# A decoder block on one core: conditioning in five steps, and products moved from GpSimd to VectorE

## Chip, cores and metric

The kernel runs on one core of a Trainium2 chip. The metric is the device time of one execution in microseconds; less is better. The kernel before takes 2488.12 us (median of three executions, 2487.45 to 2488.19).

## What is computed

One layer of a decoder block on 256 rows of 2048 channels, in float32. A conditioning vector `ada` with nine parts of 2048 comes from one row `c` and a wide weight, and modulates three sub-layers: a SwiGLU network, a token mixer, and a second SwiGLU network.

```python
cond = jax.nn.silu(c)
ada = (cond @ w_ada[l] + b_ada[l]).reshape(B, N_ADA, 1, D)
sh1, sc1, gt1, sh2, sc2, gt2, sh3, sc3, gt3 = [ada[:, i] for i in range(N_ADA)]
h = modulate(x, g_norm[l, 0], sh1, sc1)
x = x + 0.5 * gt1 * swiglu(h, w_ffn_gate[l, 0], w_ffn_up[l, 0], w_ffn_down[l, 0])
u = modulate(x, g_norm[l, 1], sh2, sc2)
q_nsa, kv_nsa, gl_nsa, q_r, k_r, v_r, g_r, ga, gb = jnp.split(u @ w_in[l], split_at, axis=-1)
o_nsa = nsa_attention(q_nsa, kv_nsa, gl_nsa, g_qk[l], cmp_pos[l], cmp_w1[l], cmp_b1[l], cmp_w2[l])
o_ret = retention(q_r, k_r, v_r, g_r, ret_gn_gain[l])
merged = jax.nn.sigmoid(ga) * (o_nsa @ w_proj_nsa[l]) + jax.nn.sigmoid(gb) * (o_ret @ w_proj_ret[l])
x = x + gt2 * (merged @ w_out[l])
h = modulate(x, g_norm[l, 2], sh3, sc3)
x = x + 0.5 * gt3 * swiglu(h, w_ffn_gate[l, 1], w_ffn_up[l, 1], w_ffn_down[l, 1])
```

`modulate` is a root-mean-square norm of each row, times `1 + scale`, plus `shift`. The attention has four groups of four heads with three branches (compressed, selected, window), each a softmax weighted by a gate.

## The kernel before

**Units.** Every weight matrix is read once, in tiles `raw` of 128x1024 (512 KB). A tile is split into a rounded part `whi` (ScalarE, L134) and a remainder `wlo` (VectorE, L135), and the activations into `ahi` and `alo` likewise. One tile with 12 matmuls of 512 columns (hi x hi, hi x lo, lo x hi; two k-tiles; two halves of 128 rows, called half 0 and half 1) is a unit below. `run` (L137) walks one list of items in which weight tiles ("w") and conditioning rows ("a") stand in the order in which SyncE loads them. Six `raw` buffers are in flight (RAW), and items are prepared at most four ahead (AHEAD, PREP). Small pieces of other work stand in the queue `micro`; one is taken after each weight unit. Each engine runs its instructions in the order in which this walk issues them, so a late one holds up what stands behind it.

**Conditioning.** `ada` (L337) multiplies 16 rows of `w_ada` by the elements of `cond` on VectorE (L347, L349), 1024 columns at a time. `ada_cols` (L367) turns the sum into columns of shift and scale. The first network starts in steps (STEPS, `early` at L602): nine chunks of 512 columns run over k-tiles 0 to 3 (18 units), then over k-tiles 4 to 7, and so on; between steps the sums of each chunk are stored (L634) and put back into PSUM (L640) by ScalarE. `first` (L693) makes the conditioning and the modulated activations of a step (`mk`: L736, L737 on ScalarE, L741 on VectorE). `interleave` (L421) spreads the 16 conditioning rows of the next step over the first 95% of a step's units (SPREAD), and `mk` comes after the last of them.

**The norms between the sub-layers.** The last chunk (`tail` in `chunk`, L228) finishes half 0 two units early, so that the row factors of half 0 (L326, GpSimd) are made beside the matmuls of half 1. `norm` (L475) brings them to all partitions by a matmul (L483), multiplies the transposed x (L496 on VectorE for the first 512 channels, L521 on GpSimd for the rest) and makes `ahi` and `alo` (L499, L502, L525, L526). The first two units of the following chunk (HOLD) run on half 0 alone; `head` then makes half 1 and releases their matmuls for half 1. `x_scaled` (L458) transposes 512 channels of x (L454, 8 transposes) and scales them.

**Attention.** For each group the list `steps` at L1097 stands in `micro`. `scores` makes masked scores, `softmax` (L1041) exponentials on ScalarE and, through `weigh` (L967), the product with gate and reciprocal sum on GpSimd (L971, L1050); `c_softmax` (L992) does so for the compressed branch (L998, L1003); `p_tr` (L1053) transposes and splits (L1063, L1064), `pv` (L1068) multiplies by the values (L1078 to L1080).

Of the kernel before, what the change touches and what calls it, by code (L numbers as in the profile page):

```python
# [32 lines left out]
RAW, PREP, AHEAD, T4, T2, EARLY, SPREAD = (6, 4, 4, 6, 8, 9, 0.95)  # L33
# [14 lines left out]
STEPS = ((0, 4), (4, 4), (8, 4), (12, 4))  # L48
# [23 lines left out]
def block_kernel(ctx: ExitStack, tc: tile.TileContext, I, konst, decay, out):  # L72
# [43 lines left out]
    items, micro, held, first_lo = [], deque(), [], []  # L116
# [20 lines left out]
    def run():  # L137
# [11 lines left out]
        def dma():  # L149
            while st["dma"] < len(stream) and (st["dma"] < RAW or st["dma"] - RAW in freed):  # L150
                i = st["dma"]
                _, src, nk, n, _ = stream[i]
# [11 lines left out]
        def prep():  # L164
            i = st["prep"]
            kind, _, nk, n, fn = stream[i]
            raw = raws.pop(i)
            if kind == "w":
                hi = wp.tile([P, 2 * NCH], F32R, tag="whi", name="whi")
                lo = wp.tile([P, 2 * NCH], F32R, tag="wlo", name="wlo")  # L170
                if st["w"]:
                    split(raw[:, :nk * n], hi[:, :nk * n], lo[:, :nk * n])
                else:
                    nc.scalar.activation(hi[:, :nk * n], raw[:, :nk * n], AF.Copy)
                    first_lo.append(lambda: nc.vector.tensor_tensor(
# [10 lines left out]
        at, nw = 0, 0  # L186
        for it in items:
# [4 lines left out]
            if kind == "bar":  # L192
                bars.pop(0)
                continue
            while st["prep"] < len(stream) and st["prep"] <= at + AHEAD and (not bars or st["prep"] < bars[0]):
# [32 lines left out]
    def chunk(act, src, K, n, done, nk=2, banks=accb, head=None, tail=None):  # L228
# [29 lines left out]
        return its[:h0] + ([("bar", HOLD[2])] if head else []) + its[h0:]  # L258
# [108 lines left out]
    def ada_cols(lay, k0, nk=4, first=False):  # L367
# [12 lines left out]
        def done(acc):  # L380
            if first:
# [3 lines left out]
                finish(ps[:, 0:2 * nk].rearrange("p (i k) -> p i k", i=2))  # L385
                return
# [79 lines left out]
    def rstd_diag(t):  # L466
# [3 lines left out]
        rsqrt_mean(r, r, D)  # L470
        dg = t2([P, P])
# [3 lines left out]
    def norm(xa, his, los, dgs):  # L475

        box = []

        def rows_of(t):
            if not t:  # L480
                box.append(mx([P, 2, S])[:, 0])
            r = box[0][:, t * P:(t + 1) * P]
            nc.tensor.matmul(r, ones, dgs[t], start=True, stop=True)  # L483
            return r

        def half(t):
            r = rows_of(t)
            ts = slice(t * P, (t + 1) * P)
            if not t:
                his.append(act_hi())  # L490
                los.append(act_lo())
            h = xa[0]

            def scaled(b):
                hb = h[:, 2 * b:2 * b + 2, ts]
                nc.vector.tensor_tensor(hb, hb, r[:, None, :].to_broadcast([P, 2, P]), op=ALU.mult)  # L496

            def hi(k):
                nc.scalar.activation(his[0][:, k, ts], h[:, k, ts], AF.Identity, bias=mod[:, 0, k:k + 1])  # L499

            def lo(k):
# [191 lines left out]
    def first(k0, nk):  # L693
# [602 lines left out]
```

## Time and profile before

| | before |
|---|---|
| median of three executions | 2488.12 us |
| the profiled execution, its own time | 2489.26 us |
| its span, first to last instruction | 2487.5 us |
| TensorE matmuls busy | 2432.4 us (98%) |
| VectorE busy | 1724.6 us (69%) |
| ScalarE busy | 1202.7 us (48%) |
| GpSimd busy | 233.0 us (9%) |
| moved by DMA | 616.65 MB, mean 248 GB/s |
| mean granted TensorE clock | 0.998 |

The busy share of an engine is a mean over stages with different limits. TensorE's matmuls overlap: each lasts 380 ns and one starts every 0.216 us, so its idle time is read from gaps between starts. The profile gives, for an instruction that waited, the time that its engine sat idle and what ended it.

### The profile page before, as it was taken

How to read it: one execution, taken by the hardware profiler on the slowest of the kernel's cores; microseconds unless marked ns; L12 is line 12 of the kernel's file. 1: busy time of each engine (PE TensorE's matmuls, PEld its weight loads, DVE VectorE, ACT ScalarE, POOL GpSimd, SP SyncE). 2: the span in 40 equal slices, each digit the busy share in tenths (PEclk: the TensorE clock that was granted, in tenths of full speed). 3: DMA queues.
4: the chain of work that ended last, by engine and by line, in shares of the span. 5: the costliest groups of instructions: out<-in, count | busy, mean ns of one | idle time of the engine just before them, and what ended most of it. 6: DMA issues, size and time to landing. Idle time of an engine off the chain costs nothing. (4 is left out here: it accounts for less than half of the span.)

```text
span 2487.5 us, 31657 instructions
## 1 busy us (share of the span) xinstructions
PE 2432.4 (98%) x11614; PEld 2115.6 (85%) x11614; DVE 1724.6 (69%) x1960; ACT 1202.7 (48%) x1550; POOL 233.0 (9%) x206
## 2 busy tenths in 40 slices
PE   6999999999999999999999999999899999999999
PEld 4888888888887888888888888888788888888887
DVE  7887768998756467876666777776688555555555
ACT  4777444444445455564444444444544444444443
POOL 1000000110002133320001101001200010001001
PEclk9999999999999999999999999999999999999999
DMA  9998888899876555667888787876598666666664
GB/s 349 355 354 294 277 293 299 296 319 339 276 228 185 143 146 153 202 207 264 281 267 254 251 258 250 280 267 233 168 332 326 210 203 201 197 201 202 199 202 153
DMA packets 348264, 616.65 MB, mean 248 GB/s; under 512 B 22096, under 2 KB 79926, under 8 KB 347852
## 3 DMA queue, kind: packets, MB, share of 16 engines
q1 hardware_dynamic: 347852, 614.51, 74.9%
q8 instruction: 91, 1.49, 0.3%
q14 instruction: 65, 0.53, 0.1%
q0 software_dynamic: 256, 0.12, 0.0%
HBM read 612.45 MB, written 2.10 MB: 247 GB/s over the span
## 5 line engine op out<-in xcount | busy, mean ns | idle before, releaser
L135 DVE TENSOR_TENSOR wlo<-raw,whi 128x1024 fp32r<-128x1024 f32 x864 | 1076.6, 1255 | 588.0 <-ACT whi L134 582.6
L134 ACT ACTIVATE whi<-raw 128x1024 fp32r<-128x1024 f32 x864 | 907.1, 1057 | 945.7 <-PE accb L221 722.8
L219 PE MATMUL accb<-whi,ahi 128*128 128x512 f32 x3168 | 1213.8, 383 | 5.9 <-ACT ahi L499 5.5
L220 PE MATMUL accb<-wlo,ahi 128*128 128x512 f32 x3168 | 1202.9, 380 | 3.9 <-DVE wlo L135 3.7
L221 PE MATMUL accb<-whi,alo 128*128 128x512 f32 x3168 | 1202.4, 380 | 2.4 <-DVE alo L546 1.1
L219 PEld LDWEIGHTS accb<-whi,ahi 128*128 128x128 f32 x3168 | 599.7, 189 | 90.1 <-ACT ahi L499 6.3
L220 PEld LDWEIGHTS accb<-wlo,ahi 128*128 128x128 f32 x3168 | 599.9, 189 | 89.3 <-DVE wlo L135 7.2
L221 PEld LDWEIGHTS accb<-whi,alo 128*128 128x128 f32 x3168 | 599.6, 189 | 89.3 <-DVE alo L526 1.6
L349 DVE SCALAR_TENSOR_TENSOR aacc<-raw,cond,aacc 128x1024 f32<-128x1024 f32 x270 | 354.9, 1314 | 2.0 <-DMA raw<-in_w_ada_dram 1.0
L563 POOL TENSOR_TENSOR x<-x,t 128x512 f32<-128x512 f32 x50 | 80.9, 1640 | 1383.8 <-DVE t L561 988.0
L622 PE MATMUL accb<-wlo,ahi 128*128 128x512 f32 x288 | 112.8, 392 | 2.5 <-DVE wlo L135 2.5
L623 PE MATMUL accb<-whi,alo 128*128 128x512 f32 x288 | 110.4, 383 | 2.0 <-DVE alo L741 2.0
L621 PE MATMUL accb<-whi,ahi 128*128 128x512 f32 x288 | 110.7, 384 | 0.3 <-ACT whi L134 0.2
L622 PEld LDWEIGHTS accb<-wlo,ahi 128*128 128x128 f32 x288 | 54.8, 190 | 17.5 <-DVE wlo L135 10.3
L623 PEld LDWEIGHTS accb<-whi,alo 128*128 128x128 f32 x288 | 54.8, 190 | 10.4 <-DVE alo L741 3.5
L621 PEld LDWEIGHTS accb<-whi,ahi 128*128 128x128 f32 x288 | 54.9, 191 | 9.3 <-ACT whi L134 0.9
L546 DVE TENSOR_TENSOR alo<-mx,ahi 128x512 fp32r<-128x512 f32 x52 | 33.5, 686 | 29.8 <-ACT ahi L545 29.8
L545 ACT ACTIVATE ahi<-mx 128x512 fp32r<-128x512 f32 x52 | 28.2, 596 | 49.8 <-PE mx L454 49.8
L561 DVE TENSOR_TENSOR t<-accb,gt 128x512 f32<-128x512 f32 x56 | 36.2, 684 | 7.3 <-PE accb L221 7.3
L580 ACT ACTIVATE t<-accb 128x512 f32<-128x512 f32 x44 | 26.1, 599 | 25.6 <-PE accb L221 21.1
L1160 POOL TENSOR_SCALAR rs<-bmv 128x2 f32<-128x2 f32 x8 | 1.8, 221 | 375.8 <-DVE bmv L1159 375.5
L807 ACT ACTIVATE t<-accb 128x512 f32<-128x512 f32 x44 | 25.9, 597 | 22.7 <-PE accb L221 22.7
(202 smaller groups left out, 1094.5 us busy)
## 6 DMA issues: line engine op xcount, KB each, us to landing
raw<-in_w_ada_dram SPq DMA_DIRECT2D x288, 512.0 KB, 5.5
raw<-in_w_ffn_gate_dram SPq DMA_DIRECT2D x176, 512.0 KB, 5.3
raw<-in_w_ffn_up_dram SPq DMA_DIRECT2D x176, 512.0 KB, 4.6
raw<-in_w_ffn_down_dram SPq DMA_DIRECT2D x176, 512.0 KB, 4.4
raw<-in_w_in_dram SPq DMA_DIRECT2D x176, 512.0 KB, 4.5
raw<-in_w_in_dram SPq DMA_DIRECT2D x128, 256.0 KB, 3.8
raw<-in_w_proj_nsa_dram SPq DMA_DIRECT2D x32, 512.0 KB, 5.6
raw<-in_w_proj_ret_dram SPq DMA_DIRECT2D x32, 512.0 KB, 5.4
```

Source lines behind the costliest of these rows:

```text
L134: nc.scalar.activation(hi_ap, raw_ap, AF.Copy)
L135: nc.vector.tensor_tensor(lo_ap, raw_ap, hi_ap.bitcast(F32), op=ALU.subtract)
L219: nc.tensor.matmul(ps[t], xh, wh, start=kt == 0, stop=False)
L220: nc.tensor.matmul(ps[t], xh, wl, start=False, stop=False)
L221: nc.tensor.matmul(ps[t], xl, wh, start=False, stop=kt == K - 1)
L349: nc.vector.scalar_tensor_tensor(box[0], raw, k, box[0], op0=ALU.mult, op1=ALU.add)
L546: nc.vector.tensor_tensor(lo[:, 2 * b:2 * b + 2], ps, h.bitcast(F32), op=ALU.subtract)
L561: nc.vector.tensor_tensor(in_two(y), halves(ps[t]), in_two(gt[:, n * NCH:(n + 1) * NCH]), op=ALU.mult)
L563: (nc.vector if last and n == 3 else nc.gpsimd).tensor_tensor(xs, xs, y, op=ALU.add)
L621: nc.tensor.matmul(ps[t], xh, wh, start=kt + a == 0, stop=False, **kw)
L622: nc.tensor.matmul(ps[t], xh, wl, start=False, stop=False, **kw)
L623: nc.tensor.matmul(ps[t], xl, wh, start=False, stop=kt + a == k0 + nk - 1, **kw)
```

## The change

Four things change. First, the conditioning of the first network goes in five steps of 2, 2, 4, 4 and 4 k-tiles: the first two steps use rows of 512 columns (256 KB) and have nine units each. The rows of a step all come before the last three units of the preceding step (REST), and its shift, scale and activations (`by_ones`, `whole`, `low`) are queued after those last units and after the first unit of the step. The first step's `xs` is scaled for its own k-tiles alone. Second, in the norms all products go to VectorE, by halves and by pairs of k-tiles (`by_row`); three sets of transposes (`x_scaled(1)`, `x_turned(2)`, `x_turned(3)`) stand beside the norm's matmuls; the remainder of the third unit's weights is made after half 1's activations; and five items after it prepare one weight tile each (SLOW). The product by the gate for half 1 (`by_gate`) and its sum with x (`plus`) are separate pieces. Third, the clearing of two tiles (`clear`) goes 60 items forward. Fourth, the softmax products of attention go to VectorE, one step after the exponentials. The diff, cut to its core:

```diff
-RAW, PREP, AHEAD, T4, T2, EARLY, SPREAD = (6, 4, 4, 6, 8, 9, 0.95)
+RAW, PREP, AHEAD, T4, T2, EARLY, REST = (6, 4, 4, 6, 8, 9, 3)
...
-WARM = (10, 15, 4)
+WARM = (9, 12, 4)
...
-POOLN = 0
-O1 = ((0, 0), (0, 1), (1, 0), (1, 1), (1, 2), (1, 3), (2, 0), (2, 1), (2, 2), (2, 3))
-O0 = ((0, 0), (0, 1), (1, 0), (1, 1), (1, 2), (1, 3), (2, 0), (2, 1), (3, 0), (2, 2), (2, 3), (3, 0))
-ORDER = (O0, O1)
+SLOW = 5
 HOLD = (2,2,1)
 LATE = 4
 GAPS = (2, 4, 3, 2)
-STEPS = ((0, 4), (4, 4), (8, 4), (12, 4))
+STEPS = ((0, 2), (2, 2), (4, 4), (8, 4), (12, 4))
...
-                if st["w"]:
+                if st["w"] and len(stream[i]) == 5:
...
+                few = SLOW if len(it) > 2 else 0
...
+                if few and done:
+                    break
+                done += stream[nxt][0] == "w"
                 prep()
+            few = max(few - 1, 0)
...
-        return its[:h0] + ([("bar", HOLD[2])] if head else []) + its[h0:]
+        if head:
+            its[h0] += ("late",)
+        return its[:h0] + ([("bar", HOLD[2], "slow")] if head else []) + its[h0:]
...
-            if first:
+            def by_ones():
                 ps = mx()
                 for k in range(2 * nk):
                     nc.tensor.matmul(ps[:, k:k + 1], acc[:, k * P:(k + 1) * P], ones[:, 0:1], start=True, stop=True)
                 finish(ps[:, 0:2 * nk].rearrange("p (i k) -> p i k", i=2))
+            if then is not None:
+                if k0 == 0:
+                    by_ones()
+                else:
+                    soon(by_ones, *then)
                 return
...
-                    w = interleave(w, first(*STEPS[i + 1]), int(len(w) * SPREAD), *LEAD)
+                    w = interleave(w, first(*STEPS[i + 1]), len(w) - REST, *LEAD)
...
+        def by_row(n, b, t):
+
+            ts = slice(t * P, (t + 1) * P)
+            hb = xa[n][:, 2 * b:2 * b + 2, ts]
+            nc.vector.tensor_tensor(hb, hb, box[0][:, None, ts].to_broadcast([P, 2, P]), op=ALU.mult)
...
+                pending.pop(0)()
+            nc.tensor.matmul(box[0][:, ts], ones, diag(r2[t]), start=True, stop=True)
+            turned[turn] = x_turned(turn)
+            if t:
+                by_row(2, 0, 0)
...
+            for b in range(2):
+                by_row(0, b, t)
+            for k in range(4):
+                nc.scalar.activation(his[0][:, k, ts], xa[0][:, k, ts], AF.Identity, bias=mod[:, 0, k:k + 1])
+            lo(0)
+            lo(1)
+            if not t:
+                pending.pop(0)()
+            lo(2)
+            lo(3)
+            if not t:
+                pending.pop(0)()
+
...
         def at_once():
-            half(0)
+            xa.append(x_scaled(1))
+            half(0, 2)
+            by_row(1, 0, 0)
+            by_row(1, 1, 0)
+            xa.append(x_scaled(2, turned[2]))
             drain()
 
         def head():
-            half(1)
-            rs.append(t2([P, S]))
-            nc.scalar.activation(rs[0], box[0], AF.Copy)
-            push(part(1), part(2), lambda: xa.append(x_scaled(3)), part(3))
+            half(1, 3)
+            part(1, ((0, 1), (1, 1)))()
+            while late_lo:
+                late_lo.pop()()
+            xa.append(x_scaled(3, turned[3]))
+            push(lambda: lo_of(1), part(2, ((1, 0), (0, 1), (1, 1))), lambda: lo_of(2),
+                 part(3, ((0, 0), (1, 0), (0, 1), (1, 1))), lambda: lo_of(3))
         return at_once, head
...
-            pending.append(lambda: add_x(ps, 3, lambda t, n: None, (1,)))
+            y = []
+            pending.append(lambda: y.append(by_gate(ps, 3, 1)))
+            pending.append(lambda: plus(y[0], 3, 1, nc.vector))
...
+        then = [lambda: whole(0, 2), lambda: (low(), whole(2, 2)), low] if nk == 4 else [lambda: whole(0, 2), low]
+        o = ada_cols(0, k0, nk, then)
+        o.insert(12, ("do", turn))
+        o.insert(8, ("do", scaled))
+        if k0 == STEPS[1][0]:
+            o.insert(5, ("do", load_more))
+        return o
...
-                dgs.append(rstd_diag(t))
-            elif t == 1:
+                rs.append(rstd(t))
+            elif t == 1 and n == 0:
                 push(*[None] * GAPS[2], lambda: xa.append(x_scaled(n)))
...
+            items.insert(len(items) - 60, ("do", lambda: clear()))
...
-            nc.gpsimd.tensor_tensor(sums, sums, gate, op=ALU.mult)
+            nc.vector.tensor_tensor(sums, sums, gate, op=ALU.mult)
...
-                nc.gpsimd.tensor_tensor(pv[:, t], pv[:, t], mask_c[:, t, None, :].to_broadcast([P, 4, NCMP]), op=ALU.mult)
+                nc.vector.tensor_tensor(pv[:, t], pv[:, t], mask_c[:, t, None, :].to_broadcast([P, 4, NCMP]), op=ALU.mult)
...
-            nc.gpsimd.tensor_tensor(p3, p3, s8[:, :, None].to_broadcast([P, 8, NCMP]), op=ALU.mult)
+            weigh(sv, gates[:, :, 4 * g:4 * g + 4])
+            nc.vector.tensor_tensor(p3, p3, s8[:, :, None].to_broadcast([P, 8, NCMP]), op=ALU.mult)
...
-                nc.gpsimd.tensor_tensor(s, s, sums[:, :, None].to_broadcast([P, 4, n]), op=ALU.mult)
+                weigh(sums, gates[:, t, c0:c0 + 4])
+                nc.vector.tensor_tensor(s, s, sums[:, :, None].to_broadcast([P, 4, n]), op=ALU.mult)
...
-        steps = [k_tr, None, None, None, q_tr, c_scores, scores(1, 1), both(softmax(1, 1), scores(0, 1)),
-                 both(softmax(0, 1), c_softmax), both(scores(1, 0), scores(0, 0)),
-                 both(p_tr(1, 1), c_split, softmax(1, 0), softmax(0, 0)), None, both(pv(1, (1,), False), p_tr(0, 1)), c_tr,
-                 both(pv(1, (0,), True), p_tr(1, 0), p_tr(0, 0)), None, pv(0, (1, 0), True)]
+        steps = [k_tr, None, None, None, q_tr, c_scores, both(c_exp, scores(1, 1)), both(exps(1, 1), scores(0, 1)),
+                 both(c_norm, weighed(1, 1), exps(0, 1)), both(weighed(0, 1), c_split, scores(1, 0), scores(0, 0)),
+                 both(p_tr(1, 1), exps(1, 0), exps(0, 0)), both(weighed(1, 0), weighed(0, 0)),
+                 both(pv(1, (1,), False), p_tr(0, 1)), c_tr, both(pv(1, (0,), True), p_tr(1, 0), p_tr(0, 0)), None,
+                 pv(0, (1, 0), True)]
```

**ScalarE, end of the step that precedes k-tiles 4 to 7.** L640/L673 puts a chunk's sums back, L634/L667 stores them, L736/L762 and L737/L763 make activations. Before (the last rows of `mk`):

```order
L737 ACTIVATE t_695<-mx,mod 128x256
L736 ACTIVATE ahi<-mx,mod 128x256
L737 ACTIVATE t_695<-mx,mod 128x256
L634 ACTIVATE t_716<-accb 128x512 x2
L134 ACTIVATE whi<-raw 128x1024
L640 ACTIVATE accb<-alo 128x512 x2
L134 ACTIVATE whi<-raw 128x1024
```

In the change:

```order
L673 ACTIVATE accb<-alo 128x512 x2
L667 ACTIVATE ahi<-accb 128x512 x2
L673 ACTIVATE accb<-t_508 128x512 x2
L667 ACTIVATE alo<-accb 128x512 x2
L762 ACTIVATE ahi<-mx,mod 128x256
L763 ACTIVATE t_763<-mx,mod 128x256
L762 ACTIVATE ahi<-mx,mod 128x256
L763 ACTIVATE t_763<-mx,mod 128x256
L131 ACTIVATE whi<-raw 128x1024
L673 ACTIVATE accb<-ahi 128x512 x2
```

Four of the eight activations now stand between the storing of the last chunk but one and the putting back of the first chunk's sums (the L673 row at the end); the other four come after that.

**VectorE, first norm, from half 1's product on.** L496/L501 is the product by the row factors, L502/L516 and L526/L539 make `alo`, L135/L132 and L172 `wlo`. Before:

```order
L496 TENSOR_TENSOR t_5887<-t_5887,mx 128x2x128 x2
L502 SCALAR_TENSOR_TENSOR alo<-t_5887,mod,ahi 128x128 x4
L526 SCALAR_TENSOR_TENSOR alo<-t_6030,mod,ahi 128x256 x4
L135 TENSOR_TENSOR wlo<-raw,whi 128x1024 x3
L526 SCALAR_TENSOR_TENSOR alo<-t_6165,mod,ahi 128x256 x4
L135 TENSOR_TENSOR wlo<-raw,whi 128x1024 x2
L526 SCALAR_TENSOR_TENSOR alo<-t_6385,mod,ahi 128x256 x4
L135 TENSOR_TENSOR wlo<-raw,whi 128x1024 x3
L830 COPY t_6487<-mx 128x512 x2
L837 TENSOR_TENSOR t_6500<-t_6487,cols 128x960
```

In the change:

```order
L516 SCALAR_TENSOR_TENSOR alo<-t_5983,mod,ahi 128x128 x4
L501 TENSOR_TENSOR t_6303<-t_6303,mx 128x2x128 x2
L172 TENSOR_TENSOR wlo<-raw,whi 128x1024
L539 SCALAR_TENSOR_TENSOR alo<-t_6303,mod,ahi 128x256 x4
L132 TENSOR_TENSOR wlo<-raw,whi 128x1024
L501 TENSOR_TENSOR t_6345<-t_6345,mx 128x2x128 x3
L132 TENSOR_TENSOR wlo<-raw,whi 128x1024
L539 SCALAR_TENSOR_TENSOR alo<-t_6345,mod,ahi 128x256 x4
L132 TENSOR_TENSOR wlo<-raw,whi 128x1024
L501 TENSOR_TENSOR t_6403<-t_6403,mx 128x2x128 x4
L132 TENSOR_TENSOR wlo<-raw,whi 128x1024
L539 SCALAR_TENSOR_TENSOR alo<-t_6403,mod,ahi 128x256 x4
```

The products of L521 on GpSimd have become rows of VectorE between the weights' remainders, which now come one at a time.

**VectorE, first group's softmax.** L1034/L1076 makes scores, L1000/L1042 sums the compressed branch, L970/L1010 takes reciprocals, L1098 is the product by gate and sum. Before:

```order
L969 TENSOR_SCALAR s_7411<-s_7411 128x4
L970 RECIPROCAL s_7411<-s_7411 128x4
L1000 TENSOR_REDUCE s_7423<-pc 128x8
L969 TENSOR_SCALAR s_7423<-s_7423 128x8
L970 RECIPROCAL s_7423<-s_7423 128x8
L135 TENSOR_TENSOR wlo<-raw,whi 128x1024
L1034 SCALAR_TENSOR_TENSOR t_7450<-kc,mx 128x128 x4
L1037 TENSOR_REDUCE m_7460<-t_7450 128x4
L1034 SCALAR_TENSOR_TENSOR t_7462<-kc,mx 128x128 x4
L1037 TENSOR_REDUCE m_7472<-t_7462 128x4
```

In the change:

```order
L1040 TENSOR_TENSOR pc<-pc,kc 128x60 x2
L1042 TENSOR_REDUCE s_7498<-pc 128x8
L1009 TENSOR_SCALAR s_7498<-s_7498 128x8
L1010 RECIPROCAL s_7498<-s_7498 128x8
L1011 TENSOR_TENSOR s_7498<-s_7498,gates 128x8
L1045 TENSOR_TENSOR pc<-pc,s_7498 128x120
L1009 TENSOR_SCALAR s_7435<-s_7435 128x4
L1010 RECIPROCAL s_7435<-s_7435 128x4
L1011 TENSOR_TENSOR s_7435<-s_7435,gates 128x4
L1098 TENSOR_TENSOR t_7404<-t_7404,s_7435 128x1024
L132 TENSOR_TENSOR wlo<-raw,whi 128x1024
L1009 TENSOR_SCALAR s_7508<-s_7508 128x4
```

The sum of the compressed branch stood behind a product on GpSimd; now that product (L1040) and those by the gate (L1011, L1045, L1098) are VectorE's own.

## Rows read from the trace of the kernel before

**Rows 1.** The page, busy time, share of the span and instructions.

```profile
PE 2432.4 (98%) x11614; PEld 2115.6 (85%) x11614; DVE 1724.6 (69%) x1960; ACT 1202.7 (48%) x1550; POOL 233.0 (9%) x206
```

**Rows 2.** Busy time by stretch; after POOL: granted clock, DMA share, GB/s.

```profile
10.00:20.00 10.00, 1.36 (x3) 0.55 (x3) 8.17 (x11) 3.80 (x10) 3.04 (x2) 1.00 1.05 387
...
842.00:864.00 22.00, 22.00 (x129) 19.25 (x128) 9.15 (x18) 10.32 (x14) 3.25 (x5) 1.00 0.43 126
```

**Rows 3.** Timeline of the start: start, duration (us), engine, line, [idle before].

```profile
15.50 17.55 DVE L349 SCALAR_TENSOR_TENSOR aacc<-raw,cond,aacc 128x1024 f32<-128x1024 f32 x13
...
33.05 1.06 ACT L174 ACTIVATE whi<-raw 128x1024 fp32r<-128x1024 f32 x1 [9.28 <-DMA raw<-in_w_ffn_gate_dram]
...
33.11 1.95 PE L384 MATMUL mx<-ones,aacc 128*128 128x1 f32 x16 [1.04 <-DVE aacc L349]
...
36.16 0.48 PE L621 MATMUL accb<-whi,ahi 128*128 128x512 f32 x1
```

**Rows 4.** A group of the page: count, busy us, mean ns, idle before.

```profile
L561 DVE TENSOR_TENSOR t<-accb,gt 128x512 f32<-128x512 f32 x56 | 36.2, 684 | 7.3 <-PE accb L221 7.3
```

**Rows 5.** Timeline of ScalarE within and at the end of the second step.

```profile
111.17 1.06 ACT L134 ACTIVATE whi<-raw 128x1024 fp32r<-128x1024 f32 x1 [0.66 <-DMA raw<-in_w_ffn_gate_dram]
112.14 1.10 ACT L640 ACTIVATE accb<-ahi 128x512 f32<-128x512 f32 x2
...
143.04 0.58 ACT L736 ACTIVATE ahi<-mx,mod 128x256 fp32r<-128x256 f32 x1
143.49 0.58 ACT L737 ACTIVATE t<-mx,mod 128x256 f32<-128x256 f32 x1
```

**Rows 6.** TensorE, timeline at two places, and its waits in total (us, times, longest).

```profile
92.75 0.48 PE L623 MATMUL accb<-whi,alo 128*128 128x512 f32 x1 [0.17 <-DVE alo L741]
...
167.93 0.48 PE L622 MATMUL accb<-wlo,ahi 128*128 128x512 f32 x1 [0.63 <-DVE wlo L135]
...
PE accb L623 <- DVE alo L741: 2.0, 3, 1.4
```

**Rows 7.** Timeline of the two norms.

```profile
753.42 1.04 PE L454 MATMUL mx<-kc,x 128*128 128x128 f32 x8
...
769.72 1.23 DVE L135 TENSOR_TENSOR wlo<-raw,whi 128x1024 fp32r<-128x1024 f32 x1 [0.70 <-ACT whi L134]
...
770.87 0.75 DVE L496 TENSOR_TENSOR t<-t,mx 128x256 f32<-128x256 f32 x2
...
771.77 0.80 PE L219 MATMUL accb<-whi,ahi 128*128 128x512 f32 x1 [2.20 <-ACT ahi L499]
...
793.62 0.38 PE L221 MATMUL accb<-whi,alo 128*128 128x512 f32 x1
...
1785.68 0.48 PE L219 MATMUL accb<-whi,ahi 128*128 128x512 f32 x1 [1.41 <-ACT ahi L499]
...
1793.04 1.69 ACT L525 ACTIVATE ahi<-t,mod 128x256 fp32r<-128x256 f32 x4
...
1796.19 1.66 DVE L526 SCALAR_TENSOR_TENSOR alo<-t,mod,ahi 128x256 fp32r<-128x256 f32 x4
...
1807.55 0.38 PE L221 MATMUL accb<-whi,alo 128*128 128x512 f32 x1
```

**Rows 8.** VectorE's waits in total.

```profile
DVE s L1000 <- POOL pc L998: 16.7, 4, 6.6
```

**Rows 9.** Timeline of the first two groups' softmax.

```profile
918.32 0.28 DVE L1000 TENSOR_REDUCE s<-pc 128x8 f32<-128x120 f32 x1 [6.61 <-POOL pc L998]
...
920.20 0.48 PE L220 MATMUL accb<-wlo,ahi 128*128 128x512 f32 x1 [1.24 <-DVE wlo L135]
...
924.96 0.48 PE L1079 MATMUL mx<-t,t 128*128 128x512 f32 x1 [1.90 <-DVE t L1064]
...
987.07 0.48 PE L1079 MATMUL mx<-t,t 128*128 128x512 f32 x1 [1.64 <-DVE t L1064]
```

**Rows 10.** Busy time in the third group's softmax.

```profile
1040.00:1062.00 22.00, 21.70 (x115) 18.67 (x115) 20.38 (x49) 15.70 (x36) 8.85 (x11) 1.00 0.67 205
```

More of the change, by code (lines that the diff above doesn't have):

```diff
@@ L113, in in_two @@
         return ap.rearrange("p (h j) -> p h j", h=2)
-    items, micro, held, first_lo = [], deque(), [], []
+    items, micro, held, late_lo = [], deque(), [], []
     def weights(src, nk, n, fn):
@@ L185, in run @@
         dma()
[L186 removed]
+        at, nw, few = 0, 0, 0
         for it in items:
@@ L365, in over_partitions, with ada_cols @@
         return halves(ps)
-    def ada_cols(lay, k0, nk=4, first=False):
+    def ada_cols(lay, k0, nk=4, then=None):
         ks = slice(k0, k0 + nk)
@@ L473, in rstd_diag, with norm, half @@
         return dg
-    def norm(xa, his, los, dgs):
-        box = []
-        def rows_of(t):
+    def norm(xa, his, los, r2):
+        box, turned = [], {}
+        def by_row(n, b, t):
+            ts = slice(t * P, (t + 1) * P)
+            hb = xa[n][:, 2 * b:2 * b + 2, ts]
+            nc.vector.tensor_tensor(hb, hb, box[0][:, None, ts].to_broadcast([P, 2, P]), op=ALU.mult)
+        def half(t, turn):
+            ts = slice(t * P, (t + 1) * P)
             if not t:
                 box.append(mx([P, 2, S])[:, 0])
[L482 to L489, printed above, removed]
@@ new lines, in half, with hi_of @@
+            for k in range(4):
[8 more added lines that the diff above has]
+                pending.pop(0)()
+        def hi_of(n):
+            his.append(act_hi())
+            for k in range(4):
+                nc.scalar.activation(his[n][:, k], xa[n][:, k], AF.Identity, bias=mod[:, 0, 4 * n + k:4 * n + k + 1])
@@ L528, in part, with lo_of @@
+        def lo_of(n):
+            los.append(act_lo())
+            for k in range(4):
+                nc.vector.scalar_tensor_tensor(los[n][:, k], xa[n][:, k], mod[:, 0, 4 * n + k:4 * n + k + 1],
+                                               his[n][:, k].bitcast(F32), op0=ALU.add, op1=ALU.subtract)
+        def part(n, whats):
+            def f():
+                for b, t in whats:
+                    by_row(n, b, t)
+                hi_of(n)
             return f
-        rs = []
         def at_once():
-            half(0)
+            xa.append(x_scaled(1))
[3 more added lines that the diff above has]
+            xa.append(x_scaled(2, turned[2]))
@@ L1039, in scores, with exps, f, weighed @@
             return f
-        def softmax(br, t):
+        def exps(br, t):
+            def f():
+                s, m = box["p", br, t], box["m", br, t]
+                sums = sp.tile([P, 4], F32, tag="s4", name="s4", bufs=4)
+                for h in range(4):
+                    nc.scalar.activation(s[:, h], s[:, h], AF.Exp, bias=m[:, h:h + 1], accum_out=sums[:, h:h + 1])
+                box["s", br, t] = sums
+            return f
+        def weighed(br, t):
             def f():
                 n = P * (t + 1)
-                s, m = box["p", br, t], box["m", br, t]
-                sums = small(4, "s4")
-                for h in range(4):
-                    nc.scalar.activation(s[:, h], s[:, h], AF.Exp, bias=m[:, h:h + 1], accum_out=sums[:, h:h + 1])
+                s, sums = box["p", br, t], box["s", br, t]
                 c0 = 16 * (1 + br) + 4 * g
-                weigh(s, sums, gates[:, t, c0:c0 + 4], 4)
-                nc.gpsimd.tensor_tensor(s, s, sums[:, :, None].to_broadcast([P, 4, n]), op=ALU.mult)
+                weigh(sums, gates[:, t, c0:c0 + 4])
+                nc.vector.tensor_tensor(s, s, sums[:, :, None].to_broadcast([P, 4, n]), op=ALU.mult)
             return f
@@ L1258, in block_kernel @@
     h3, l3 = [], []
-    at_once, head = norm(xa3, h3, l3, dg3)
+    at_once, head = norm(xa3, h3, l3, r3_)
     items.append(("do", at_once))
```

155 lines of the change are left out of this document (65 added, 90 removed).

## The prediction

> **What bounds the kernel now.** I read the busy line of the page first [rows 1]: TensorE's matmuls fill 98% of the span, so a microsecond saved on another engine counts only where TensorE waits. Next the timeline of TensorE, for gaps between starts: it stands idle for the main work until 36.16 us [rows 3], and then in stalls at the steps' ends [rows 6], at the two norms [rows 7] and in attention [rows 9]. One unit is 12 matmuls, one each 0.216 us, 2.59 us. The sum is made against the profiled execution (2489.26 us), 1.14 us over the median of three (2488.12). Some 0.2% (5 us) is what a measurement can tell from no change.
>
> **The start.** Before the first main matmul come x (2.1 MB) and 16 rows of 0.524 MB; the DMA engines are full there, at 387 GB/s [rows 2], so a row needs 1.355 us. VectorE's products keep that pace, 17.55/13 = 1.35 us each [rows 3]. The last product ends at 33.05; less itself and 27.1 us of loads, loading begins at 4.6. With half as many bytes in rows (4.2 MB) loads end at 4.6 + 16.3 = 20.9. A product of 512 columns has no row; the nearest operation of that size with two inputs takes 684 ns [rows 4], half of the 1.35, so the last one ends at about 22 to 22.6, and the 16 small matmuls (1.95 us, [rows 3]) halve. The first main matmul moves from 36.16 to about 24.7, 11 us earlier.
>
> **What the second step does with it.** The first unit of k-tiles 4 to 7 (unit 19) still needs all rows of k-tiles 0 to 7. Ahead of the last row stand x, 16.8 MB of rows and 17 weight tiles before, 15 after: 27.8 and 26.7 MB, so at the full rate it lands at 4.6 + 71.8 = 76.4 and now at 73.6. With holes, as six buffers come free only behind their users, I take 76. The second step's rows cannot hide: its first six units have 15.5 us of matmuls, and 16 rows with 6 tiles need 22 x 1.355 = 29.8 us. So TensorE waits for transfers. After the last row come its product (1.4), a first tile's landing, rounding and remainder (about 2.5), three units and the small matmuls (2). Per unit ScalarE rounds (0.97, [rows 5]), puts two sums back and stores two (1.05 each, by the 1.10 row), 3.0 us, over the 2.59. Behind the last stores it does four activations at 0.45 [rows 5], a rounding and a putting back before unit 19 can begin, 3.8 us, as its order shows. That makes 76 + 1.4 + 2.5 + 3 x 3.0 + 3.8 = 92.7, and about 93.2 with the first remainder. Before, the same unit started at about 92.5 [rows 6]: **+0.7**. At the full rate, with three units at 2.59 and nothing of ScalarE's 3.8 in the way, it is 73.6 + 1.4 + 2.5 + 7.8 = 85.3, 7.2 us earlier than before: the bound on the good side. At the three boundaries before, the waits for `alo` add up to 2.0 us, and the wait for the weights' remainder beside one adds 0.63 [rows 6]; with activations made over the three units ahead, I estimate 1.3 less in all. **Early part: -0.6.**
>
> On the other side, 256-KB rows have no row in the trace. The slowest nearby stretch moves 126 GB/s at a busy share of 0.43 [rows 2], 293 at full share; 8.4 MB of rows (both steps) at 293 instead of 387 cost 6.9 us. I take nothing, because with six transfers in flight the 512-KB rows already fill the engines. The Trainium skill (DMA: Bandwidth & Descriptors, Measured (HBM→SBUF, 128 partitions, SWDGE, issued from GpSimd)) wants transfers of 1 MiB or more for three quarters of the peak; read between its sizes, 256 KB would do some 62% where 512 KB do 73%, an estimate that costs 3.8 us; no run here shows 256 KB yet.
>
> **The norms.** Two sets of 8 transposes leave TensorE's busy time for idle gaps, about 0.8 us each (row of 753.42, [rows 7]): -1.6 per norm. The third set lies within the next figure. Release: half 1's held matmuls start at 771.77 and 1785.68 [rows 7]. At the first, a weights' remainder (1.23) stands ahead of half 1's products on VectorE; held back now, and with the gate's product in a piece of its own (0.7 sooner), this gives 2.0; at the second norm, where the chain was shorter, about 1.1. After the release: before, unit 8 ended 21.9 us later both times (793.62, 1807.55). Now what GpSimd did beside joins VectorE and alternates with ScalarE. VectorE from the release: lows 1.3, products (0.375 each by [rows 7]) until 2.0, held remainder 3.2, four lows (1.66) 4.9; unit 4's remainder waits until 5.9 for its rounding, behind eight activations on ScalarE (1.69 per four), and ends at 7.1; products 8.2; ScalarE's four activations and a rounding, 10.6; remainder 11.8; lows 13.4; remainder and four products 16.1; activations and rounding 18.8; remainder and lows 21.6; the last unit ends at 24.5. So +2.6. First norm -1.6 - 2.0 + 2.6 = **-1.0**, second -1.6 - 1.1 + 2.6 = **-0.1**; I allow 3 each way, a chain of this length being worth one remainder and one set of lows either way.
>
> **Attention.** VectorE stands 16.7 us in four waits for GpSimd's product of the compressed branch, the longest 6.6 [rows 8]; in the first group it delays a weights' remainder (TensorE waits 1.24) and the transposed softmax (1.90), in the second 1.64 [rows 9]. These waits go. In their place VectorE does the products: two of 128x1024 ahead of the transposes (1.14 each, as a remainder of that size), small ones 1.1, 3.4 us per group, and 4.9 with the later ones. So VectorE comes to the transposes earlier by 4.2 us with the smaller waits in the first group, and by 1.5, 0.5 and 0.6 in the others. Counted by starts, TensorE's gaps there are 1.39 + 2.06, 1.80, 0.71 and some 0.5; they shrink by 3.45, 1.5, 0.5 and 0.5: **-6.0**, between -7 (all gaps) and the rival below.
>
> **Sum.** -0.6 - 1.0 - 0.1 - 6.0 = -7.7: the profiled execution comes to 2481.6, the median to **2480.4 us**.
>
> **Rivals.**
> *The start's gain is kept.* If transfers stay dense and ScalarE keeps up, unit 19 starts 7.2 us earlier and not 0.7 later: 2480.4 - 7.9 = about 2472. For it: 2.7 us less to load, and only 26.7 MB to move by then. Against it: ScalarE's 3.0 us per unit, and its order at the boundary. Chance 0.18.
> *The early part loses.* Smaller rows or a ScalarE that lags cost up to 6.9 us: 2480.4 + 6.9 = about 2487, no change. Chance 0.18. The rule of the Trainium skill above would be one way to it.
> *VectorE fills up in attention* (the other side). In the third group it is busy for 20.38 of 22 us already [rows 10]. If its 4.9 us more per group find no idle time in groups two to four, weights' remainders come late behind them: 3 x 4.9 - 3.45 = +11.3, in place of -6.0, 2480.4 + 17.3 = 2497.7. It decides once VectorE lags more than the four units prepared ahead (10.4 us); +6.7 in attention is enough for slower by 0.2%. Against it: it had idled 16.7 us there, and 0.3 us more in each group does not make a lag of ten. Chance 0.05.
> *The change does not do what it says*: the order shows 512-column rows, the products on VectorE and the moved activations, so I give it nothing of its own.
>
> **Chances and range.** The forecast itself has 0.59; its own range, 2475 to 2486, is the norms' allowance and the early part's smaller errors. Of it 0.49 lies beyond 0.2% and 0.10 within; the first rival is faster, the second 0.02 faster, 0.14 within and 0.02 slower, the third slower. Faster 0.69, same 0.24, slower 0.07. Range **2468 to 2488**: it reaches to both early rivals and leaves out the third.
>
> **What would show it.** Right: the first main matmul at about 24.7; TensorE and DMA waits between it and unit 19, which starts near 93; ScalarE nearly full before; releases at about 2 and 1 us less, and unit 8 ending 24 to 25 us behind them; L1042 with no wait for GpSimd, and no wait of L1127 for the transposed softmax. Wrong: unit 19 under 89 or over 97; unit 8 within 22 us of the release; waits of TensorE for `wlo` in the second to fourth group's softmax.

## The result and the profile after

The change made the kernel slower: 2502.31 us (median of 6; 2500.21 to 2503.86) against 2488.15 (6 runs of the kernel before), a ratio of 1.0051, interval 1.0041 to 1.0061. The forecast was 2480.4, with 2488 as the upper end. The profiled execution took 2502.37 us with a span of 2500.2, 12.7 more than before.

The same step in both traces shows where. The lag of the change behind the kernel before is -9.4 us at the first main matmul (26.77 for 36.16), +13.0 in unit 19, the first of k-tiles 4 to 7 (its first matmul with `alo`: 105.76 for 92.75), +14.4 when the gates of the first network are made (467 us), +15.4 ahead of the first norm and +16.7 behind it, +12.3 behind attention, and +12.4 behind the second norm and at the end. The reading at 467 us is on the low side. Both traces have 10368 main matmuls (those that write `accb`), so the n-th of one can be set beside the n-th of the other. Counted so, the lag is +16.7 us throughout from 210 to 450 us of the kernel before, for example here, first before and then in the change:

```profile
293.11 0.38 PE L219 MATMUL accb<-whi,ahi 128*128 128x512 f32 x1
```

```profile
309.77 0.38 PE L222 MATMUL accb<-whi,ahi 128*128 128x512 f32 x1
```

It falls to +13.9 at 510 us and is back at +15.4 by 589. All runs below gain 0.8 to 2.8 us from 450 to 510, and attention_alone, whose code up to attention is that of the kernel before, gains 2.8 as well; so the fall comes from the one execution of the kernel before and not from the change. The early part lost 16.7 by this count, the first norm 1.3, attention gave back 4.4, and the second norm changed nothing.

The page's busy line and busy time by stretch, columns as in [rows 1, 2]:

```profile
PE 2440.4 (98%) x11610; PEld 2119.7 (85%) x11610; DVE 1744.3 (70%) x2049; ACT 1220.9 (49%) x1586; POOL 170.0 (7%) x146
```

```profile
10.00:20.00 10.00, 4.56 (x9) 2.18 (x10) 8.63 (x16) 3.38 (x10) 1.91 (x2) 1.00 1.03 322
20.00:25.00 5.00, 4.30 (x13) 1.85 (x12) 3.71 (x6) 0.00 (x0) 0.00 (x0) 1.00 0.78 237
25.00:55.00 30.00, 23.86 (x88) 17.55 (x88) 22.04 (x28) 17.73 (x27) 0.00 (x0) 0.89 0.99 330
65.00:75.00 10.00, 6.96 (x28) 4.64 (x26) 9.81 (x9) 7.31 (x14) 0.00 (x0) 1.00 0.83 266
1052.00:1074.00 22.00, 21.79 (x118) 19.00 (x117) 21.04 (x49) 14.87 (x34) 0.00 (x0) 1.00 0.58 170
```

TensorE is busy for 98% as before, and that says nothing. The last two columns do: loading at the start ran at 387 GB/s [rows 2] and now runs at 237 to 330 in these four stretches, with a DMA share of 0.78 to 1.03. Against 387, they lack 0.65 + 0.75 + 1.71 + 1.21 = 4.3 MB, 11.2 us of loading. The kernel before was not at 387 throughout either (352 from 25 to 55 us). From 10 to 90 us it moved 29.75 MB and the change 26.56, 3.2 MB less, which is 8.2 us at 387; first before, then the change:

```profile
DMA packets 15558, 29.75 MB, mean 372 GB/s; under 512 B 926, under 2 KB 1182, under 8 KB 15553
```

```profile
DMA packets 18064, 26.56 MB, mean 332 GB/s; under 512 B 1070, under 2 KB 9173, under 8 KB 18059
```

The timeline of the start, and of the end of the second step (as [rows 3, 5, 6]):

```profile
13.53 10.24 DVE L354 SCALAR_TENSOR_TENSOR aacc<-raw,cond,aacc 128x512 f32<-128x512 f32 x13
23.82 1.05 PE L389 MATMUL mx<-ones,aacc 128*128 128x1 f32 x8 [0.70 <-DVE aacc L354]
26.77 0.79 PE L654 MATMUL accb<-whi,ahi 128*128 128x512 f32 x1 [0.86 <-ACT ahi L762]
...
87.60 1.28 DVE L354 SCALAR_TENSOR_TENSOR aacc<-raw,cond,aacc 128x1024 f32<-128x1024 f32 x1
88.88 1.06 ACT L131 ACTIVATE whi<-raw 128x1024 fp32r<-128x1024 f32 x1 [1.74 <-DMA raw<-in_w_ffn_gate_dram]
...
100.49 0.60 ACT L667 ACTIVATE alo<-accb 128x512 f32<-128x512 f32 x1 [0.70 <-PE accb L656]
100.98 0.56 ACT L762 ACTIVATE ahi<-mx,mod 128x256 fp32r<-128x256 f32 x1
...
102.78 1.07 ACT L131 ACTIVATE whi<-raw 128x1024 fp32r<-128x1024 f32 x1
103.72 1.14 ACT L673 ACTIVATE accb<-ahi 128x512 f32<-128x512 f32 x2
...
104.39 0.48 PE L654 MATMUL accb<-whi,ahi 128*128 128x512 f32 x1 [1.35 <-ACT accb L673]
105.76 0.48 PE L656 MATMUL accb<-whi,alo 128*128 128x512 f32 x1 [0.67 <-DVE alo L768]
```

The last row of k-tiles 4 to 7 is multiplied by 88.9 us, not by 77.4 as forecast; from there to unit 19 the order on ScalarE is the forecast one.

The slow stretch from 65 to 75 us holds no short rows: every transfer issued in it has 512 KB. It stands behind the boundary that the change adds, between its two short steps (unit 10):

```profile
61.51 0.58 ACT L763 ACTIVATE t<-mx,mod 128x256 f32<-128x256 f32 x1
...
63.95 1.09 ACT L131 ACTIVATE whi<-raw 128x1024 fp32r<-128x1024 f32 x1
...
65.08 1.22 DVE L132 TENSOR_TENSOR wlo<-raw,whi 128x1024 fp32r<-128x1024 f32 x1 [2.27 <-ACT whi L131]
```

ScalarE is busy without a gap from 60 to 70 us, with four activations and the sums of that boundary, so the weights' rounding is late; VectorE waits for it with landed rows in line behind, and is then busy for 9.81 of 10 us. Meanwhile buffers come free late, and the DMA share falls to 0.73 (65 to 70).

At the last boundary something comes that was not forecast:

```profile
209.83 0.58 ACT L763 ACTIVATE t<-mx,mod 128x256 f32<-128x256 f32 x1
210.28 2.02 ACT L131 ACTIVATE whi<-raw 128x1024 fp32r<-128x1024 f32 x2
...
211.39 2.36 DVE L132 TENSOR_TENSOR wlo<-raw,whi 128x1024 fp32r<-128x1024 f32 x2 [3.54 <-ACT whi L131]
213.66 0.68 DVE L768 TENSOR_TENSOR alo<-t,ahi 128x512 fp32r<-128x512 f32 x1
214.40 0.79 PE L656 MATMUL accb<-whi,alo 128*128 128x512 f32 x1 [3.43 <-DVE alo L768]
214.99 0.63 PE L654 MATMUL accb<-whi,ahi 128*128 128x512 f32 x1
```

The second pair's activations are done at about 210.3, but their remainder (L768) stands on VectorE behind two weights' remainders, which wait for two roundings behind those activations. TensorE idles 3.43 us, and afterwards a matmul lasts 0.63 us in place of 0.38: the granted clock is 0.83 over 210 to 220, so some 3.4 us at 1.2 GHz.

The norms (TensorE; release and end of unit 8, as [rows 7]) and attention (VectorE, then TensorE, as [rows 8, 9]):

```profile
783.80 0.48 PE L222 MATMUL accb<-whi,ahi 128*128 128x512 f32 x1 [0.47 <-ACT ahi L521]
...
802.24 0.48 PE L222 MATMUL accb<-whi,ahi 128*128 128x512 f32 x1 [1.04 <-ACT whi L131]
...
810.22 0.38 PE L224 MATMUL accb<-whi,alo 128*128 128x512 f32 x1
...
1795.46 0.48 PE L222 MATMUL accb<-whi,ahi 128*128 128x512 f32 x1 [0.47 <-ACT ahi L521]
...
1819.92 0.38 PE L224 MATMUL accb<-whi,alo 128*128 128x512 f32 x1
...
927.70 0.28 DVE L1042 TENSOR_REDUCE s<-pc 128x8 f32<-128x120 f32 x1
...
938.83 0.48 PE L1127 MATMUL mx<-t,t 128*128 128x512 f32 x1 [0.54 <-DVE t L1112]
```

TensorE's wait there in total (us, times, longest):

```profile
PE mx L1127 <- DVE t L1112: 1.6, 4, 0.5
```

L1042 no longer waits for GpSimd, and the weights' remainder that TensorE waited for at 920.20 is in time.

### The profile page after: what moved, and what is told of

Its sections match the earlier page's. It is cut to its first block, busy times and chain, and to the rows that moved or that the text cites. A ratio compares the mean times of both kernels' runs of the same rounds, so it can differ in the third digit from the quotient of the medians.

```text
span 2500.2 us, 31727 instructions
## 1 busy us (share of the span) xinstructions
PE 2440.4 (98%) x11610; PEld 2119.7 (85%) x11610; DVE 1744.3 (70%) x2049; ACT 1220.9 (49%) x1586; POOL 170.0 (7%) x146
## 5 line engine op out<-in xcount | busy, mean ns | idle before, releaser
L132 DVE TENSOR_TENSOR wlo<-raw,whi 128x1024 fp32r<-128x1024 f32 x862 | 1069.0, 1249 | 609.8 <-ACT whi L131 603.4
L354 DVE SCALAR_TENSOR_TENSOR aacc<-raw,cond,aacc 128x1024 f32<-128x1024 f32 (+1 forms) x285 | 357.3, 1254 | 2.0 <-DMA raw<-in_w_ada_dram 0.8
L654 PE MATMUL accb<-whi,ahi 128*128 128x512 f32 x288 | 114.0, 396 | 10.7 <-ACT accb L673 7.3
L656 PEld LDWEIGHTS accb<-whi,alo 128*128 128x128 f32 x288 | 56.2, 195 | 13.7 <-DVE alo L768 5.9
L1088 ACT ACTIVATE t<-t,m 128x256 f32<-128x256 f32 (+1 forms) x64 | 28.2, 444 | 18.5 <-DVE m L1079 18.5
```

What stands on the lines that cost most here:

```text
L132: nc.vector.tensor_tensor(lo_ap, raw_ap, hi_ap.bitcast(F32), op=ALU.subtract)
L354: nc.vector.scalar_tensor_tensor(box[0], raw, k, box[0], op0=ALU.mult, op1=ALU.add)
L654: nc.tensor.matmul(ps[t], xh, wh, start=kt + a == 0, stop=False, **kw)
L656: nc.tensor.matmul(ps[t], xl, wh, start=False, stop=kt + a == k0 + nk - 1, **kw)
```

## The experiments

The first column of times is the median of the run and, behind the stroke, of the kernel before beside it. The lag is that of the first row of the gates (466.74 us before, 481.11 in the change) and holds the early part alone; two kernels whose early part is that of before show -1.1 and -2.1, so a single lag at that row is good to some 2 us. The last column is the lag by the count of main matmuls, at 293 us of the kernel before; there the same two show +0.4 and -0.1.

| run | us / before | ratio, interval | early lag, us | by matmuls, us |
|---|---|---|---|---|
| the change | 2502.31 / 2488.15 | 1.0051 (1.0041 to 1.0061) | +14.4 | +16.7 |
| steps_of_four | 2491.66 / 2490.34 | 1.0006 (0.9996 to 1.0015) | +6.8 | +8.1 |
| early_undone | 2485.83 / 2490.34 | 0.9982 (0.9972 to 0.9991) | -1.1 | +0.4 |
| long_packets | 2500.78 / 2490.34 | 1.0046 (1.0031 to 1.0061) | +13.7 | +16.0 |
| attention_alone | 2484.13 / 2490.34 | 0.9980 (0.9970 to 0.9990) | -2.1 | -0.1 |
| pairs | 2495.16 / 2490.47 | 1.0019 (1.0009 to 1.0028) | +8.9 | +10.7 |
| at_once | 2499.99 / 2490.47 | 1.0041 (1.0026 to 1.0056) | +13.5 | +14.7 |
| four_low | 2487.88 / 2490.47 | 0.9990 (0.9981 to 1.0000) | +2.8 | +3.7 |
| raw7 | 2500.16 / 2490.47 | 1.0039 (1.0024 to 1.0054) | +11.4 | +13.8 |
| pairs_low | 2488.81 / 2489.01 | 1.0001 (0.9991 to 1.0010) | +5.0 | +6.0 |
| pairs_long | 2494.74 / 2489.01 | 1.0023 (1.0013 to 1.0032) | +8.1 | +10.0 |
| pairs_two | 2495.10 / 2489.01 | 1.0023 (1.0014 to 1.0032) | +7.2 | +8.7 |

**Which part lost.** early_undone keeps norms and attention and takes `first`, `ada_cols`, STEPS, SPREAD and WARM from the kernel before; attention_alone is the kernel before with the attention of the change (`exps`, `weighed`, `c_norm`, `steps`).

> The change with the conditioning of the first network as before (steps of four, rows over 95% of a step, activations in one piece); norms and attention as changed. By the lags read between the two traces (about +14.4 us early, +1.3 at the first norm, -4.4 in attention, 0 to 0.3 at the second norm) it comes to 2488.15 + 1.3 - 4.4 + 0.2 = about 2485. Rival: if the norms or attention had only looked better because the early part shifted them, 2488 or more.

> The kernel before with only attention changed (products on VectorE, one step later). By the lags between the traces -4.4 us: about 2483.8. By the prediction -6.0: about 2482.2. If VectorE only gained there because it came late with other work, 2488.

Both are faster than the kernel before beside them, and so than the change. Between the scores of the first group and the end of the last one each gains: 4.3 us with the norms changed, 4.1 without. Attention gains whether VectorE is late or not; the norms add nothing that can be measured.

**Steps of four, all else as in the change.**

```diff
-STEPS = ((0, 2), (2, 2), (4, 4), (8, 4), (12, 4))
+STEPS = ((0, 4), (4, 4), (8, 4), (12, 4))
```

> The change with STEPS back at 4, 4, 4, 4; rows still end three units before a step does (REST) and the activations are still spread. Theory A (the two steps of two k-tiles, their short packets and their rows, are the whole early loss): the loss of about 14.5 us goes, and the time is that of the kernel with the whole early part undone, about 2485, within 1 us. Theory B (rows that end three units early cost by themselves, since loading is at its limit before the first boundary): the first boundary comes some 4 to 5 us later than in the kernel before (unit 19 started there at about 92.3), and the time is about 2489 to 2490.

Neither theory has it all: half the loss (14.4 to 6.8, or 16.7 to 8.1 by matmuls) goes with the short steps, and the rest stays. Part of that rest is this run's own. WARM still puts the warm-up matmuls (L750) behind the rows that suit the short step, and 16 long rows take longer:

```profile
27.34 1.91 PE L750 MATMUL mx<-raw,ones 128*128 128x512 f32 x2
33.29 3.57 PE L389 MATMUL mx<-ones,aacc 128*128 128x1 f32 x16 [4.03 <-DVE aacc L354]
```

TensorE idles 4.03 us, the granted clock is 0.66 from 30 to 40 us (0.85 before), the 16 small matmuls take 3.57 us in place of 1.95 [rows 3], and the first main matmul starts at 38.57, 2.4 us later than before. The run four_low below has this too.

The trace has the same 3.43 us wait for `alo` at the last boundary. That led to four_low:

```diff
...
-[lambda: whole(0, 2), lambda: (low(), whole(2, 2)), low]
+[lambda: whole(0, 2), lambda: (low(), whole(2, 2), low())]
...
```

> Steps of four with the spread activations, except that the remainder of the second pair of k-tiles is made right behind its activations and not one unit later. Theory A (at the last boundary that remainder stands on VectorE behind two weights' remainders whose rounding waits behind eight activations; TensorE idles 3.4 us for it and then runs at 1.2 GHz for some 6 us): the wait at 204.6 falls from 3.43 to about 1 us, no stretch at half clock follows, and the time falls from 2491.7 by 4 to 6 us to about 2487. Theory B (the remainder is late because its activations are late): the wait stays over 2.5 us and the time at 2490 to 2492.

Theory A holds. The place in TensorE's timeline:

```profile
203.02 0.48 PE L656 MATMUL accb<-whi,alo 128*128 128x512 f32 x1 [0.21 <-DVE alo L768]
```

The granted clock is 1.00 from 200 to 220 us. The lag falls by 4.0 us (4.4 by matmuls); so the order of one remainder, with the slow clock behind its wait, cost some 4 in the run with steps of four. In the change itself the lag by matmuls grows by 3.5 over the last boundary, from 13.2 to 16.7.

**Why loading is slow.** Three runs change how the short rows are loaded. long_packets reads 512 adjacent columns, so that a packet has 2 KB and not 1 KB:

```diff
...
+            if nk == 2:
+                return w[:, k0 * 2 * P:(k0 + 2) * 2 * P][:, None, :]
```

> The change, except that the rows of the two short steps are read as 512 adjacent columns (2 KB a packet) in place of 256 of shift and 256 of scale (1 KB each); bytes, transfers and instructions are the same in number. The conditioning of k-tiles 0 to 3 so comes from other columns. Theory A (the 1-KB packets are what slows loading: 6.4 of the 11.4 us by which the last row is late): the rate from 10 to 60 us rises from about 300 to 350 to some 380 GB/s, unit 19 (104.4 us in the change) starts 5 to 6 us earlier, and the time falls to about 2496. Theory B (too few bytes in six buffers, or VectorE's pace): unit 19 moves by less than 2 us and the time stays at 2500 to 2502.

pairs puts two rows into one buffer; the places of the warm-up and of the other small work in the list move with them:

```diff
+        if width == 2 * P:
+            def pair(kt):
+                return lambda raw: [step(kt + a)(raw[:, a * 2 * width:(a + 1) * 2 * width]) for a in range(2)]
+            its = [("a", src(w_ada[kt * P:(kt + 2) * P, :]), 2, 2 * width, pair(kt)) for kt in range(0, KT, 2)]
...
```

> The change, except that two rows of the two short steps share one raw buffer (two transfers of 256 KB into its halves), so that up to twelve short transfers are in flight in place of six; packets (1 KB), bytes and products are the same. Theory A (six buffers hold too few bytes of short rows, so loading runs at 300 to 350 GB/s instead of 387): the rate between 25 and 60 us rises to 370 or more, unit 19 (104.4 us in the change) starts 4 to 6 us earlier and the time falls from 2502 to about 2497. Theory B (VectorE's product of 512 columns, 0.79 us, or the 1-KB packets set the pace): rate and unit 19 stay within 2 us, and the time at 2500 to 2502.

raw7 has RAW = 7 and T2 = 6.

> The change with seven raw buffers in place of six, and six 128x512 scratch buffers in place of eight to make room. Theory A (bytes in flight bound the loading of the short steps): the last row of k-tiles 4 to 7 is multiplied 2 to 3 us earlier than at 88.9 us, and the time falls to about 2499. Theory B (not the number of buffers): unit 19 stays within 1 us of 104.4; 2501 to 2503, or more if the scratch buffers are missed.

Busy time from 10 to 55 us, first of the change with long packets, then with pairs, then with seven buffers:

```profile
10.00:55.00 45.00, 32.42 (x107) 21.37 (x108) 33.16 (x47) 18.57 (x33) 1.91 (x2) 0.92 0.91 302
```

```profile
10.00:55.00 45.00, 33.74 (x139) 25.67 (x140) 38.15 (x54) 25.59 (x44) 1.90 (x2) 0.96 1.07 365
```

```profile
10.00:55.00 45.00, 31.62 (x114) 21.83 (x115) 35.00 (x49) 22.17 (x38) 1.91 (x2) 0.96 1.01 331
```

The change itself moved 318 GB/s there. Longer packets lower the busy share and not the time (the matmul with `alo` in unit 19 at 105.20 for 105.76): the packets did not bound, and theory A of that run falls. Twice as many short rows under way bring 365 GB/s and that matmul at 97.44, 8.3 us earlier: theory A of pairs holds. One buffer more brings 331 GB/s and 1.8 us (103.94), between the two theories of raw7; that is less than its share (318 x 7/6 = 371). Its time is no better for it because of its missing scratch buffers: attention gives nothing back in it, with ten waits at L1127 in place of four. So what six buffers keep under way bounded the loading of the short rows: 13 of the 15 transfers issued from 10 to 25 us, and 13 of 26 from 25 to 55, fill a buffer only by half.

pairs changes one thing more: items are prepared four ahead (AHEAD), and a pair is one item, so more is prepared early. The change's trace speaks against this as the reason. In the first step ScalarE waits for the landing of each weight tile from the second on (seven waits of 0.27 to 3.03 us), and not for its turn, for example:

```profile
42.67 1.06 ACT L131 ACTIVATE whi<-raw 128x1024 fp32r<-128x1024 f32 x1 [2.25 <-DMA raw<-in_w_ffn_gate_dram]
...
47.73 1.06 ACT L131 ACTIVATE whi<-raw 128x1024 fp32r<-128x1024 f32 x1 [3.03 <-DMA raw<-in_w_ffn_up_dram]
```

Whether a buffer is held by the transfer's own time or by products in line behind a late weight tile, no run separates. An estimate from the change's trace: 26 transfers in 30 us through six buffers hold each for 6.9 us, of which 4.2 us (256 KB) or 4.8 to 6.1 (512 KB) lie between issue and landing, by the medians.

pairs_long has pairs and long packets:

> Two short rows to a raw buffer as before, again two transfers of 256 KB, but with rows of 512 adjacent columns (2-KB packets in place of 1 KB). The conditioning of k-tiles 0 to 3 so comes from other columns. Theory A (with the buffers full, 1-KB packets cost what is left, 348 to 382 GB/s at a full share against 387): the rate from 10 to 55 us is 380 to 387, unit 19 starts 2 us earlier than 96.1 and the time is about 2493. Theory B (packets make no difference): rate and unit 19 as with pairs, 2495.

With the buffers repaired the packets can be seen. The packets of 10 to 20 us, pairs and then pairs_long:

```profile
DMA packets 3608, 3.48 MB, mean 348 GB/s; under 512 B 209, under 2 KB 3608, under 8 KB 3608
```

```profile
DMA packets 2124, 3.87 MB, mean 387 GB/s; under 512 B 237, under 2 KB 237, under 8 KB 2124
```

At full engines 1-KB packets move 348 GB/s and 2-KB packets 387, a tenth less; but unit 19 does not come earlier (its matmul with `alo` at 98.63 for 97.44), for what is gained by 25 us is lost in gaps behind it: from 25 to 55 us it moves 335 GB/s where pairs moves 371, and from 10 to 55 352 for 365. Theory B holds for the time; of theory A only the price of a packet at full engines is seen, not the rate over the whole stretch.

**What is left.** at_once has REST = 1 and calls `by_ones` and all of `then` in place of queueing them; pairs_low has both repairs; pairs_two besides has REST = 2 and all activations in one piece.

> The change, except that a step's rows end one unit before the preceding step does (REST 1) and its shift, scale and all activations follow the last row in one piece. Theory A (rows that must land three units early, and activations spread over units, are the part of the loss that steps of four with them also showed, some 6 us): unit 19 starts 3 to 5 us earlier than 104.4, the wait of 3.43 us for alo at the last boundary (214.4) falls to the 1.4 of the kernel before, and the time comes to about 2495. Theory B (only the short steps cost): 2500 to 2502.

Neither theory: the wait at the last boundary falls to 1.40 us as theory A has it, but unit 19 starts later still, at 106.86 for 104.39, because ScalarE now makes eight activations and a putting back between the shift and it:

```profile
106.86 0.79 PE L656 MATMUL accb<-whi,ahi 128*128 128x512 f32 x1 [5.42 <-ACT accb L675]
```

> The change with both repairs: two short rows to a raw buffer, and the remainder of the second pair of k-tiles right behind its activations. If the two losses are separate (7 us by the run with pairs, 4 by the run with the earlier remainder), the time is 2502.3 - 7 - 4 = about 2491, the wait for alo at the last boundary (207) falls from 3.43 to under 1 us and no half clock follows. If they overlap, 2494 to 2495.

2488.81: the two losses are separate (5.5 for the buffers and about 4 for the remainder by the lags, 6.0 and 4.7 by matmuls), and with both repaired the change is as fast as the kernel before. The early part is still 5.0 behind (6.0 by matmuls), about what attention gives.

> Both repairs, and rows that end two units before a step's end in place of three, with all activations of the step after its last unit but before its first. Theory A (each unit that the rows must land earlier costs 2.6 us where loading bounds): unit 19 2 to 3 us earlier than with the repairs alone, about 2488. Theory B (activations in one piece give that back through ScalarE, 5.4 us of wait as in the run with everything at once): 2491 to 2494.

Theory A falls; 2495.10 is slower even than theory B has it. Loading a unit less early brings unit 19 no earlier (its `alo` at 98.94 against 98.39); at each later boundary TensorE waits 1.14 us for `ahi` and 1.40 for `alo` instead.

## Why the prediction was wrong

**The start** was nearly right: 26.77 for 24.7. The product of 512 columns was mis-sized: 10.24/13 = 0.79 us and not half of 1.35, so VectorE, and not loading, set the pace (the last product ended at 23.8, not 22.6). At that pace it frees 256 KB every 0.79 us, which is 332 GB/s; from 10 to 20 us loading ran at 322.

**The step that failed is the landing of the last row of k-tiles 4 to 7.** I took 76 us for it, 2.4 over the full rate, and nothing for the short rows, "because with six transfers in flight the 512-KB rows already fill the engines". It was multiplied by 88.9 and not 77.4. Six transfers of 512 KB fill the engines; with short rows among them the same six buffers gave 237 to 330 GB/s, and the view that I read (387 GB/s with six large ones, [rows 2]) says nothing of that. I had a bound for the term (6.9 us if short rows run at 293 GB/s), gave it a chance of 0.18, and took its outcome for no change; short rows and weight tiles together ran at 318 from 10 to 55 us, and the row came 11.5 us late, more than the bound. The runs show the place: two short rows to a buffer brought 5.5 us back by the gates, 6.0 by matmuls and 8.3 at unit 19; longer packets brought 0.7 by either lag.

The rest of the delay has another place that the forecast left out. It counted ScalarE's activations and sums at unit 19, and not at the boundary that the change itself adds, at unit 10; all holes in loading together had 2.4 us. There loading moved 2.66 MB from 65 to 75 us where the kernel before moved 3.87, 3.1 us at 387, with transfers of 512 KB alone. No run changes this boundary by itself, so its share of the lag is not shown.

The Trainium skill's table (DMA: Bandwidth & Descriptors, Measured (HBM→SBUF, 128 partitions, SWDGE, issued from GpSimd)) gave, by the forecast's interpolation, an estimate of 387 x 62/73 = 329 GB/s for 256 KB, close to the measured 318. But the runs speak against transfer size as the reason: pairs_long still moves its short rows 256 KB at a time, and at 387 GB/s from 10 to 25 us.

**From the last row to unit 19** the sum holds: 104.39 - 88.9 = 15.5 us, forecast 92.7 - 77.4 = 15.3 (76 + 1.4 to 92.7).

**The later boundaries** were to gain 1.3. The first two have 0.67 and 0.38 of waiting for `alo` (0.17 and 0.45 before), and unit 19 begins with 1.35 for the sums put back; the last has 3.43 (1.39 before) and a half clock behind it, 3.5 to 4 us in all. The forecast asked whether the activations would be in time, and not what stands on VectorE between an activation and its remainder.

**The norms** came out by their working. The releases are 3.4 and 2.5 us earlier than the lag ahead of them (forecast 3.6 and 2.7); unit 8 ends 26.4 and 24.5 us behind them (forecast 24.5). Beside the 2 us too much at the first norm stands a stretch at half clock behind the wait of 1.04 at 802: the granted clock was 0.66 from 803 to 808. Of the other runs with these norms, counted by matmuls, four_low and raw7 lost 1.1 and 1.2 there as well, and the rest gained 0.3 to 0.7; so a loss there is not the rule.

**Attention** was mis-sized by a quarter: 4.4 for 6.0, by groups 2.8, 1.2, 0.4 and 0 for 3.45, 1.5, 0.5 and 0.5. A wait of 0.2 to 0.5 us for the transposed softmax stays in each group. The rival in which VectorE fills up did not come, though it was busy for 21.04 of 22 us.

So the sign was lost in one sum: -0.6 early was +14.4 at the gates, +16.7 by matmuls. Of the 16.7, 6.0 go with two short rows to a buffer, 4.7 more with the order of the remainder, and 6.0 stay when both are repaired (pairs_low). What makes up these 6.0 is open: the boundary at unit 10, one more set of sums to store and put back, and rows that must be there three units early are candidates, and they were not tried apart. pairs_two asked for rows two units early in place of three and brought unit 19 no sooner, though it moved the activations as well.

## What to carry to other kernels

Halving a transfer halves what the same number of buffers keeps under way: where loading bounds, count bytes in flight, not transfers, and put two small ones into one buffer. An earlier start was worth nothing here, because the next steps still waited for nearly the same bytes: 9.4 us ahead at the first main matmul had become 13.0 behind by unit 19. When work is cut into pieces and queued, look in the order of the consuming engine for what now stands between a piece and the piece that needs it.

## What the runs showed of the hardware

Packets of 1 KB cost a tenth of the rate at full DMA engines (348 against 387 GB/s, busy shares 1.09 and 1.05, pairs and pairs_long from 10 to 20 us). A busy share near 1 is no sign of full rate: the change's loading had 0.99 at 330 GB/s. VectorE's product with an accumulator took 0.79 us for 512 columns where 1024 took 1.35. After the 3.43 us wait of TensorE at the last boundary the granted clock stood at half for some 3 us (0.83 over 210 to 220), and without that wait it did not fall there (1.00 from 200 to 220 us in four_low and pairs_low).
